# Decays inside a chunk as products of token-major gates with 0/1 matrices, and GpSimd's tile work of the first stage on other engines

## The chip, the cores and the metric

The kernel runs on one core of one Trainium2 chip. A core has TensorE (PE; its weight loads are listed apart as PEld), VectorE (DVE), ScalarE (ACT), GpSimd (POOL) and SyncE (SP), which issues the DMAs. What counts is the device time of one execution in microseconds. A time is compared as the median of several runs; a trace shows one profiled execution.

## The reference

One layer of an encoder trunk on 2048 tokens of width 1024, all in float32. The change lies in the GLA half of the token mixer and in the projection ahead of it:

```python
xn = rms_norm(h, norm_mix_pre[i])
z = xn @ w_in[i]
...
z_rwkv = z_rwkv + rwkv_mu[i] * (centred_shift(z_rwkv) - z_rwkv)
...
log_a = jax.nn.log_sigmoid(jnp.einsum('btdr,drc->btdc', a_lo, a_up) + a_b) / GLA_GATE_TEMP
...
bc = jnp.cumsum(to_chunks(log_a), axis=-2)
def step(S, inp):
    q_c, k_c, v_c, b_c = inp
    o_inter = jnp.einsum('bhcd,bhde->bhce', q_c * jnp.exp(b_c), S)
    diff = b_c[:, :, :, None, :] - b_c[:, :, None, :, :]
    dmat = jnp.exp(jnp.where(mask, diff, -jnp.inf))
    scores = jnp.einsum('bhid,bhjd,bhijd->bhij', q_c, k_c, dmat)
    o_intra = jnp.einsum('bhij,bhje->bhie', scores, v_c)
```

There are 4 GLA heads with 64 key and 128 value channels, and two directions. An RWKV-7 mixer with 8 heads runs beside them; an output projection, a SwiGLU network and a gated embedding follow.

## The kernel before

`phase_a` is the first stage. It goes over the sequence in four quarters of 512 tokens. For each it normalizes and transposes `x` (`make_xn`), then makes 27 column blocks of the projection (`zmat`): each block is 2 x 8 steps of three float32r products (high and low parts, lines 73 to 75), evacuated by ScalarE as `z`. In the first quarter the raw weights `wr` come in halves, ScalarE rounds them to `wh` and GpSimd subtracts to get `wl` (line 218); both go to DRAM, and the later quarters load them from there (line 209).

`mixed` adds a block's neighbours in time (GpSimd, line 296) and mixes them in (VectorE, lines 297 and 298). `rwkv_pair` makes the operands of two RWKV heads, `gla` and `gla_head` those of the GLA heads. A tile of a GLA head holds the forward direction on partitions 0 to 63 and the backward one on 64 to 127. `b` is the running sum of the gates in chunks of 128 tokens. The scores inside a chunk are built in seven levels: at a level with blocks of `n` tokens the decays are `exp` of the distance of `b` from its value in the middle of a block of 2n. GpSimd makes the two differences (532, 533; 523, 524 at level 6), ScalarE the exponential (534), GpSimd multiplies with the queries (`qq`, 535), VectorE with the keys (`kz`, 536, 537), TensorE makes four 128x128 float32 products (`pl`, 540), and VectorE copies them into `sc` under a mask (544).

The generators of the two kinds of heads are interleaved by `ORDER`; within that a scheduler sets the order of each engine's queue when the program is built, and each engine then runs its queue in that order. So products of the projection (`pz`) stand between the small products of the heads. The heads of the last quarter run beside the beginning of `phase_b`, the RWKV recurrence; `phase_c` has the output projection and the rest. GpSimd also computes a triangular inverse at the beginning of `phase_b` (694, 695).

Of the kernel before, what the change touches and what calls it, by code (L numbers as in the profile page):

```python
# [7 lines left out]
F32 = mybir.dt.float32  # L8
# [4 lines left out]
ALU = mybir.AluOpType  # L13
# [75 lines left out]
def col(k, i, n=1):  # L89
    return k.pv[:, i:i + n]  # L90


def phase_a(ctx, ctr, ctb, tc, k):
# [103 lines left out]

    kz = [c.tile([128, TQ], F32, name=f"kz{li}") for li in range(7)]
# [5 lines left out]
    def weights(ft, first):  # L204
# [141 lines left out]
    def rwkv_pair(q, p, x, lo):  # L346
# [30 lines left out]
        sq = t("sq")  # L377
# [27 lines left out]
        for d in range(2):  # L405
# [6 lines left out]
            V.tensor_scalar(u, u, 1.0, None, op0=ALU.add)  # L412
# [29 lines left out]
    def gla(q, x, al):  # L442
        ts_ = slice(q * TQ, q * TQ + TQ)
        t = lambda tag, bufs=1, n=TQ: gp.tile([128, n], F32, tag=tag, bufs=bufs, name=tag)
        for i in range(2):

            ab = abp.tile([128, 2, TQ], F32, tag="ab", name="ab")
            bx = gp.tile([128, 2, TQ], F32, tag="bx", name="bx")
            for hh in range(2):
# [3 lines left out]
                S.activation(ab[:, hh], pg, AF.Abs, bias=col(k, PV_AB + h))  # L453
# [3 lines left out]
            for hh in range(2):  # L457
                V.tensor_sub(ab[:, hh], bx[:, hh], ab[:, hh])

                V.tensor_tensor_scan(bx[0:64, hh], m128[0:64], ab[0:64, hh], 0.0, op0=ALU.mult, op1=ALU.add)  # L460
                V.tensor_tensor_scan(bx[64:128, hh, ::-1], m128[64:128, ::-1], ab[64:128, hh, ::-1], 0.0, op0=ALU.mult, op1=ALU.subtract)
# [11 lines left out]
            for hh in range(2):  # L473
# [6 lines left out]
                gla_head(q, h, bx[:, hh], q2[hh], k2[hh], vt)  # L480
# [8 lines left out]
    def gla_head(q, h, b, q2, k2, vt):  # L489
# [8 lines left out]
        nc.sync.dma_start(k.d["qb"][h, :, q * TQ:q * TQ + TQ], qh[B_])  # L498
        kh = t("f", 2)
# [9 lines left out]

        sc = t("sc")  # L510
        for li in (6, 0, 1, 2, 3, 4, 5):
            pl = ps3.tile([128, 512], F32, tag="ps3", name="pl")
            n = LV[li]
            tv = lambda ap: ap.rearrange("p (b t) -> p b t", t=2 * n)
            nb = TQ // (2 * n)
            bv, k2v, kv = tv(b), tv(k2), tv(kz[li])
            lhs = kz[li]
            rhs = t("qq", 2)
            f = t("f", 2)
            if li == 6:  # L520

                fv = tv(f)
                G.tensor_sub(fv[F_], bv[F_], bv[F_, :, 0:1].to_broadcast([64, nb, 2]))
                G.tensor_sub(fv[B_], bv[B_, :, 1:2].to_broadcast([64, nb, 2]), bv[B_])
                S.activation(f, f, AF.Exp, scale=0.0625)
                G.tensor_mul(rhs, f, q2)
                V.tensor_copy(kv[F_, :, 0:1], k2v[F_, :, 0:1])
                V.tensor_copy(kv[B_, :, 1:2], k2v[B_, :, 1:2])
            else:
                mid = bv[:, :, n:n + 1].to_broadcast([128, nb, n])  # L530
                fv = tv(f)
                G.tensor_sub(fv[:, :, 0:n], mid, bv[:, :, 0:n])
                G.tensor_sub(fv[:, :, n:2 * n], bv[:, :, n:2 * n], mid)
                S.activation(f, f, AF.Exp, scale=0.0625)  # L534
                G.tensor_mul(rhs, f, q2)  # L535
                V.tensor_mul(kv[F_, :, 0:n], fv[F_, :, 0:n], k2v[F_, :, 0:n])
                V.tensor_mul(kv[B_, :, n:2 * n], fv[B_, :, n:2 * n], k2v[B_, :, n:2 * n])  # L537
# [1030 lines left out]
```

## Time and profile before

| | before |
|---|---|
| median of 3 runs | 3658.14 us (3655.13 to 3660.93) |
| profiled execution | 3649.02 us, span 3647.3 us |
| TensorE busy | 3347.8 us (92%) |
| VectorE busy | 2624.4 us (72%) |
| ScalarE busy | 1640.8 us (45%) |
| GpSimd busy | 978.7 us (27%) |
| first stage, about 40 to 1190 us | a third of the span |

Busy times come from one execution. A matmul's row has a start and a modelled end; matmuls are pipelined, so that the distance between starts tells what one costs in a row. An instruction that takes longer than another of the same form and engine was held up in itself; a wait stands in front of an instruction and is put down to the one that came last.

### The profile page before, as it was taken

How to read it: one execution, taken by the hardware profiler on the slowest of the kernel's cores; microseconds unless marked ns; L12 is line 12 of the kernel's file. 1: busy time of each engine (PE TensorE's matmuls, PEld its weight loads, DVE VectorE, ACT ScalarE, POOL GpSimd, SP SyncE). 2: the span in 40 equal slices, each digit the busy share in tenths (PEclk: the TensorE clock that was granted, in tenths of full speed). 3: DMA queues.
4: the chain of work that ended last, by engine and by line, in shares of the span. 5: the costliest groups of instructions: out<-in, count | busy, mean ns of one | idle time of the engine just before them, and what ended most of it. 6: DMA issues, size and time to landing. Idle time of an engine off the chain costs nothing.

```text
span 3647.3 us, 57330 instructions
## 1 busy us (share of the span) xinstructions
PE 3347.8 (92%) x20880; PEld 2856.6 (78%) x20880; DVE 2624.4 (72%) x4123; ACT 1640.8 (45%) x3451; POOL 978.7 (27%) x1348
## 2 busy tenths in 40 slices
PE   6888988988889899999969989999999999999998
PEld 6777877877878688898858868888788878787776
DVE  6888788788778467776763467777765566769887
ACT  5454445444444555656644453333433333324554
POOL 6854534534335144547401100000000000001112
PEclk9988999999998989999979999999999999999999
DMA  6655465465555445545255655555422234557775
GB/s 219 215 189 184 147 199 187 143 197 170 186 177 175 153 133 156 160 130 155 73 159 169 230 200 185 187 193 191 156 93 81 70 115 150 212 173 272 265 272 185
DMA packets 390439, 629.28 MB, mean 173 GB/s; under 512 B 122790, under 2 KB 223142, under 8 KB 390156
## 3 DMA queue, kind: packets, MB, share of 16 engines
q1 hardware_dynamic: 390156, 625.61, 52.3%
q8 instruction: 165, 2.70, 0.3%
q14 instruction: 118, 0.97, 0.1%
HBM read 403.18 MB, written 211.81 MB: 169 GB/s over the span
## 4 chain that ended last, share of the span: by engine, by line
PE 66%; DVE 17%; DMA 6%; ACT 5%; issue 4%; POOL 2%; SPq 1%; DVEq 0%; ACTq 0%; POOLq 0%
PE pB L73 6%; PE pB L75 6%; PE pB L74 6%; PE pA L74 5%; PE pA L75 4%; PE pA L73 4%; PE pC L74 4%; PE pC L75 4%; PE pC L73 4%; PE pg L662 3%; PE ph L781 3%; PE pf L798 2%; PE pz L75 2%; PE pz L73 2%; PE pz L74 2%
## 5 line engine op out<-in xcount | busy, mean ns | idle before, releaser
L1045 ACT CAST sh<-raws 128x512 fp32r<-128x512 f32 (+1 forms) x456 | 277.6, 610 | 667.0 <-PE pB L74 356.2
L73 PE MATMUL pz<-xh,wh 128*128 128x256 f32 (+1 forms) x1728 | 511.8, 297 | 26.7 <-ACT z L291 18.4
L75 PE MATMUL pz<-xh,wl 128*128 128x256 f32 (+1 forms) x1728 | 504.6, 295 | 6.0 <-DMA wl<-d_ws 4.1
L74 PE MATMUL pz<-xl,wh 128*128 128x256 f32 (+1 forms) x1728 | 504.5, 293 | 0.0
L1210 POOL TENSOR_TENSOR st<-st 128x1 f32<-128x1 f32 x64 | 18.0, 281 | 1631.2 <-ACT jk L1209 1630.7
L1046 DVE TENSOR_TENSOR sl<-raws,sh 128x512 fp32r<-128x512 f32 (+1 forms) x456 | 305.6, 671 | 112.9 <-ACT sh L1045 109.4
L73 PEld LDWEIGHTS pz<-xh,wh 128*128 128x128 f32 x1728 | 339.6, 197 | 40.3 <-ACT z L291 29.1
L75 PEld LDWEIGHTS pz<-xh,wl 128*128 128x128 f32 x1728 | 337.9, 197 | 15.1 <-DMA wl<-d_ws 6.8
L74 PEld LDWEIGHTS pz<-xl,wh 128*128 128x128 f32 x1728 | 340.1, 197 | 6.9 <-issue 5.8
L781 PE MATMUL ph<-x,wpi 128*128 128x128 f32 x1024 | 170.7, 295 | 8.9 <-ACT wpi L777 7.4
L73 PE MATMUL pA<-B11h,sh 128*128 128x512 f32 x360 | 147.7, 411 | 23.0 <-ACT B11h L1045 19.1
L540 PE MATMUL pl<-qq,kz 128*128 128x128 f32 x896 | 133.8, 296 | 32.4 <-DVE kz L537 30.9
L798 PE MATMUL pf<-sv,Ht 128*128 128x64 f32 x1024 | 152.3, 277 | 10.7 <-ACT sv L803 6.9
L540 PEld LDWEIGHTS pl<-qq,kz 128*128 128x128 f32 x896 | 121.2, 208 | 44.0 <-issue 30.2
L781 PEld LDWEIGHTS ph<-x,wpi 128*128 128x128 f32 x1024 | 139.8, 200 | 18.2 <-ACT wpi L777 12.9
L798 PEld LDWEIGHTS pf<-sv,Ht 128*128 128x128 f32 x1024 | 136.0, 196 | 22.5 <-ACT sv L803 10.4
L535 POOL TENSOR_TENSOR qq<-f,q 128x512 f32<-128x512 f32 x96 | 140.7, 1472 | 43.5 <-ACT f L534 24.2
L74 PE MATMUL pA<-B11l,sh 128*128 128x512 f32 x360 | 148.1, 411 | 3.3 <-DVE B11l L1046 3.3
L662 PE MATMUL pg<-ar,bk 64*128 64x128 f32 x1024 | 143.4, 297 | 6.0 <-DVE x L665 4.6
L75 PE MATMUL pA<-B11h,sl 128*128 128x512 f32 x360 | 146.7, 407 | 0.9 <-DVE sl L1046 0.9
L73 PE MATMUL pB<-T3h,sh 128*128 128x512 f32 x360 | 143.4, 398 | 0.0
L75 PE MATMUL pB<-T3h,sl 128*128 128x512 f32 x360 | 143.0, 397 | 0.0
(636 smaller groups left out, 9348.5 us busy)
## 6 DMA issues: line engine op xcount, KB each, us to landing
wh<-d_ws SPq DMA_DIRECT2D x81, 512.0 KB, 4.1
wl<-d_ws SPq DMA_DIRECT2D x81, 512.0 KB, 4.8
d_mt<-rawt SPq DMA_DIRECT2D x92, 256.0 KB, 2.5
raws<-in_ffn_gate SPq DMA_DIRECT2D x44, 512.0 KB, 4.4
raws<-in_ffn_up SPq DMA_DIRECT2D x44, 512.0 KB, 4.0
rawm<-d_mt SPq DMA_DIRECT2D x44, 512.0 KB, 8.6
d_hid<-c SPq DMA_DIRECT2D x88, 256.0 KB, 2.5
d_ar<-st SPq DMA_DIRECT2D x32, 512.0 KB, 2.9
```

Of the source, the lines that this page charges most:

```text
L73: nc.tensor.matmul(out, ah, bh, start=start, stop=False, **kw)
L74: nc.tensor.matmul(out, ah, bl, start=False, stop=False, **kw)
L75: nc.tensor.matmul(out, al, bh, start=False, stop=stop, **kw)
L535: G.tensor_mul(rhs, f, q2)
L540: nc.tensor.matmul(pl[:, js], lhs[:, js], rhs[:, js], start=True, stop=True)
L662: nc.tensor.matmul(pg[h][:, j], bk[HR[h], j], ar[HR[h], j], start=True, stop=True)
L781: nc.tensor.matmul(ph[:, h, j], w[:, h, j], x[:, j0 + j, 4 * h:4 * h + 2, :], start=True, stop=True)
L798: nc.tensor.matmul(pf[:, h, j0 + j], H[:, h, j], SV[p, d, c][:, h, j0 + j], start=True, stop=True)
L1045: nc.scalar.copy(hi, src)
L1046: nc.vector.tensor_sub(lo, src, hi.bitcast(F32))
L1210: G.tensor_add(st[:, 2:3], st[:, 0:1], st[:, 1:2])
```

## The change

- The running sum `b` stays for `qh`, `kh` and `dec`. The decays inside the chunk no longer come from it: the gates `g` (tile `ab`) are transposed to token-major form (`gt`, in the buffers of `kt`), and for levels 0 to 5 four products with a 0/1 matrix `W[:, li]` sum the right gates in PSUM (`pf`); ScalarE takes the exponential from there. Level 6 needs one gate alone, beside ones.
- The backward gates stand one column further, with a zero beside them, in a tile of 513 columns. So `Abs` and a subtraction run in halves.
- `decay` is called one level ahead of its use. `kh` and its transposes move behind the levels.
- VectorE makes `qq`, `wl` and the sum of neighbours; ScalarE makes the product with `mu1` and adds 1 to `u`.
- The raw weights have two buffers instead of three; `sq` uses the buffers of `out`.

```diff
+    W = c.tile([128, 6, 128], F32, name="W")
...
+        V.tensor_sub(wv[:, :, 0:n], mid, lv[:, :, 0:n])
+        V.tensor_sub(wv[:, :, n:2 * n], lv[:, :, n:2 * n], mid)
...
-            wr = wp.tile([128, n, 128], F32, tag="wr", bufs=3, name="wr")
+            wr = wp.tile([128, n, 128], F32, tag="wr", bufs=2, name="wr")
...
-            G.tensor_sub(wl[:, js], wr, wh[:, js].bitcast(F32))
+            V.tensor_sub(wl[:, js], wr, wh[:, js].bitcast(F32))
...
-        G.tensor_add(s, z[:, 0:TQ], z[:, 2:TQ + 2])
-        V.tensor_scalar(out, z[:, 1:TQ + 1], mu1[:, i:i + 1], None, op0=ALU.mult)
+        S.activation(out, z[:, 1:TQ + 1], AF.Copy, scale=mu1[:, i:i + 1])
+        V.tensor_add(s, z[:, 0:TQ], z[:, 2:TQ + 2])
...
-        sq = t("sq")
+        sq = t("out", 2)
...
-            V.tensor_scalar(u, u, 1.0, None, op0=ALU.add)
+            S.activation(u, u, AF.Identity, bias=k.one)
...
+            gr = ((slice(0, 64), slice(0, TQ)), (slice(64, 128), slice(1, TQ + 1)))
...
-                S.activation(ab[:, hh], pg, AF.Abs, bias=col(k, PV_AB + h))
+                for r, o in gr:
+                    S.activation(ab[r, hh, o], pg[r], AF.Abs, bias=col(k, PV_AB + h)[r])
...
+        gt = t("kt", 1)
+        tokmajor(g, gt, ps3, "ps3")
+
+        def decay(li):
...
+            pf = ps3.tile([128, 512], F32, tag="ps3", name="pf")
+            for j in range(4):
+                js = slice(128 * j, 128 * j + 128)
+                nc.tensor.matmul(pf[:, js], gt[:, js], W[:, li], start=True, stop=True)
+            f = t("f", 2)
+            S.activation(f, pf, AF.Exp, scale=0.0625)
+            return f
...
+            f = nxt
+            if i < 6:
+                nxt = decay(levels[i + 1])
+            fv = tv(f, n)
+            V.tensor_mul(rhs, f, q2)
...
-                G.tensor_sub(fv[:, :, 0:n], mid, bv[:, :, 0:n])
-                G.tensor_sub(fv[:, :, n:2 * n], bv[:, :, n:2 * n], mid)
-                S.activation(f, f, AF.Exp, scale=0.0625)
-                G.tensor_mul(rhs, f, q2)
```

How the order moves, first on TensorE at the end of the second quarter: the levels of its last head beside the transposes of the next quarter's `x` (`xt`). `v`, `pa`, `pss` belong to an RWKV pair. Before:

```order
L263 MATMUL pt<-ident,xt 128x128 x8
L540 MATMUL pl<-qq,kz_262 128x128 x4
L263 MATMUL pt<-ident,xt 128x128 x4
L540 MATMUL pl<-qq,kz_263 128x128 x4
L263 MATMUL pt<-ident,xt 128x128 x8
L305 MATMUL pt<-ident,v 128x128 x4
L372 MATMUL pa<-ta,aup 128x512
L373 MATMUL pa<-ta,aupl 128x512
L540 MATMUL pl<-qq,kz_264 128x128 x4
```

Now the same place, from the transposes of the gates (`ab`) on:

```order
L315 MATMUL pt<-ident,ab 128x128 x4
L273 MATMUL pt<-ident,xt 128x128 x4
L390 MATMUL pss<-out,bo 128x512
L534 MATMUL pf<-W,kt 128x128 x4
L560 MATMUL pl<-qq,kz_283 128x128 x4
L534 MATMUL pf<-W,kt 128x128 x4
L273 MATMUL pt<-ident,xt 128x128 x4
L560 MATMUL pl<-qq,kz_277 128x128 x4
L534 MATMUL pf<-W,kt 128x128 x4
L560 MATMUL pl<-qq,kz_278 128x128 x4
L534 MATMUL pf<-W,kt 128x128 x4
```

Each level now has a group `pf` ahead, a level earlier than it is used, and the head starts later against the transposes of `x`.

GpSimd's queue in the second quarter, in the middle of a head, before:

```order
L535 TENSOR_TENSOR qq<-f,q_3745 128x512
L296 TENSOR_TENSOR s<-z 128x512
L532 TENSOR_TENSOR f<-bx 128x32x8
L533 TENSOR_TENSOR f<-bx 128x32x8
L535 TENSOR_TENSOR qq<-f,q_3745 128x512 x2
```

And the rest of the second quarter now:

```order
L428 MEMSET E 128x8 x2
L526 MEMSET f 128x512 x2
L428 MEMSET E 128x8 x2
L526 MEMSET f 128x512
L428 MEMSET E 128x8 x3
L246 TENSOR_TENSOR st<-st,mhalf 128x1 x3
```

The sum of neighbours (296) stood between the levels' work; only memsets and the norms' `pow` are left. VectorE's queue at the levels of that last head now:

```order
L550 TENSOR_TENSOR qq<-f,q_5190 128x512
L555 TENSOR_TENSOR kz_279<-f,k_5261 64x16x16
L556 TENSOR_TENSOR kz_279<-f,k_5261 64x16x16
L564 COPY_PREDICATED sc<-msk,pl 128x512
L402 TENSOR_TENSOR P_6460<-kr,ta 64x512
L403 TENSOR_TENSOR P_6459<-kr,ta 64x512
L550 TENSOR_TENSOR qq<-f,q_5190 128x512
```

`qq` stands there in front of the two `kz` of its level; before, a level had two `kz` and the masked copy on this engine.

## Rows read from the trace of the kernel before

**Rows 1.** The page's part 1, and GpSimd's row of part 2.
```profile
PE 3347.8 (92%) x20880; PEld 2856.6 (78%) x20880; DVE 2624.4 (72%) x4123; ACT 1640.8 (45%) x3451; POOL 978.7 (27%) x1348
...
POOL 6854534534335144547401100000000000001112
```

**Rows 2.** Stretches: us; busy PE, PEld, DVE, ACT, POOL (instructions); clock; DMA share; GB/s.
```profile
47.00:341.00 294.00, 246.37 (x1696) 223.56 (x1695) 245.41 (x286) 149.87 (x286) 190.90 (x160) 0.91 0.58 193
341.00:615.00 274.00, 244.72 (x1754) 223.46 (x1753) 219.94 (x302) 127.22 (x244) 119.27 (x116) 0.94 0.55 176
40.00:1130.00 1090.00, 956.32 (x6806) 867.67 (x6804) 874.56 (x1156) 520.03 (x989) 518.41 (x475) 0.94 0.57 184
```

**Rows 3.** Who TensorE waits for, 70 to 1130 us: us, times, longest.
```profile
PE pl L540 <- DVE kz L537: 30.9, 19, 4.5
PE pt L305 <- DVE v L298: 18.6, 6, 5.8
PE pz L73 <- ACT z L291: 17.4, 8, 3.2
...
PE po L557 <- DVE SF L558: 9.3, 8, 2.4
...
PE pz L75 <- POOL wl L218: 1.8, 3, 0.9
...
PE pt L305 <- DVE f L503: 0.2, 1, 0.2
```

**Rows 4.** VectorE, ns min/median/max; last row, 40 to 1130 us: busy us, mean ns.
```profile
L537 DVE TENSOR_TENSOR kz<-f,k x96: 418/423/1452, 94.2 to 1177.8; 64x256 f32<-64x256 f32 x96
...
L297 DVE TENSOR_SCALAR v<-z,mu x16: 486/1010/1414, 118.0 to 1045.0; 128x512 f32<-128x512 f32 x16
...
L402 DVE TENSOR_TENSOR out<-pb,v x16: 676/688/692, 148.9 to 1082.8; 128x512 f32<-128x512 f32 x16
...
L503 DVE TENSOR_TENSOR f<-f,k x16: 659/682/1762, 91.7 to 1139.3; 128x512 f32<-128x512 f32 x16
...
L537 DVE TENSOR_TENSOR kz<-f,k 64x256 f32<-64x256 f32 x88 | 64.8, 736 | 2.5
```

**Rows 5.** GpSimd's groups up to 1500 us: busy us, mean ns | idle before.
```profile
L535 POOL TENSOR_TENSOR qq<-f,q 128x512 f32<-128x512 f32 x96 | 140.7, 1472 | 43.5 <-ACT f L534 24.2 <-PE pl L540 19.1 <-ACT u L411 0.2
...
L532 POOL TENSOR_TENSOR f<-bx 128x256 f32<-128x256 f32 x96 | 88.7, 924 | 123.2 <-PE pt L305 62.2 <-DVE kz L537 59.1
...
L533 POOL TENSOR_TENSOR f<-bx 128x256 f32<-128x256 f32 x96 | 78.8, 821 | 0.0
```

**Rows 6.** TensorE in order of time: start us, us.
```profile
151.19 0.28 PE L75 MATMUL pz<-xh,wl 128*128 128x258 f32 x1
151.31 1.06 PE L540 MATMUL pl<-qq,kz 128*128 128x128 f32 x8
152.12 0.48 PE L408 MATMUL pu<-tw,wup 128*128 128x512 f32 x1
...
664.37 0.41 PE L73 MATMUL pz<-xh,wh 128*128 128x256 f32 x1
664.58 0.36 PE L74 MATMUL pz<-xl,wh 128*128 128x256 f32 x1
...
665.24 0.60 PE L305 MATMUL pt<-ident,qk 128*128 128x128 f32 x4
665.60 0.36 PE L73 MATMUL pz<-xh,wh 128*128 128x256 f32 x1
665.80 0.28 PE L74 MATMUL pz<-xl,wh 128*128 128x256 f32 x1
```

**Rows 7.** A scaled pass of ScalarE, ns min/median/max.
```profile
L435 ACT ACTIVATE cv<-z,pv x32: 706/722/728, 63.5 to 1123.7; 128x512 f32<-128x512 f32 x32
```

**Rows 8.** The raw weights' loads, us to landing; SyncE's wait for them: us, times, longest.
```profile
wr<-in_w_in SPq DMA_DIRECT2D x45, 256.0 KB, 3.8
...
SPq L216 <- POOL wl L218: 25.0, 18, 5.2
```

More of the change, by code (lines that the diff above doesn't have):

```diff
@@ L196, in phase_a @@
         prev = cur
+    W = c.tile([128, 6, 128], F32, name="W")
+    L = pp.tile([128, TQ], F32, tag="u", bufs=2, name="L")[:, :128]
+    G.memset(L, 1.0)
+    G.affine_select(L, L, pattern=[[1, 128]], compare_op=ALU.is_ge, fill=0.0, base=0, channel_multiplier=-1)
+    for li in range(6):
+        n = LV[li]
+        lv, wv = L.rearrange("p (b t) -> p b t", t=2 * n), W[:, li].rearrange("p (b t) -> p b t", t=2 * n)
+        mid = lv[:, :, n:n + 1].to_broadcast([128, 64 // n, n])
+        V.tensor_sub(wv[:, :, 0:n], mid, lv[:, :, 0:n])
+        V.tensor_sub(wv[:, :, n:2 * n], lv[:, :, n:2 * n], mid)
     kz = [c.tile([128, TQ], F32, name=f"kz{li}") for li in range(7)]
@@ L498, in gla_head @@
         nc.sync.dma_start(k.d["qb"][h, :, q * TQ:q * TQ + TQ], qh[B_])
+        sc = t("sc")
+        tv = lambda ap, n: ap.rearrange("p (b t) -> p b t", t=2 * n)
+        gt = t("kt", 1)
+        tokmajor(g, gt, ps3, "ps3")
+        def decay(li):
+            if li == 6:
+                f = t("f", 2)
+                G.memset(f, 1.0)
+                fv = tv(f, 1)
+                S.activation(fv[F_, :, 1:2], g[F_, 0:TQ].rearrange("p (b t) -> p b t", t=2)[:, :, 1:2], AF.Exp, scale=0.0625)
+                S.activation(fv[B_, :, 0:1], g[B_, 1:TQ + 1].rearrange("p (b t) -> p b t", t=2)[:, :, 0:1], AF.Exp, scale=0.0625)
+                return f
[3 more added lines that the diff above has]
+                nc.tensor.matmul(pf[:, js], gt[:, js], W[:, li], start=True, stop=True)
+            f = t("f", 2)
+            S.activation(f, pf, AF.Exp, scale=0.0625)
+            return f
+        levels = (6, 0, 1, 2, 3, 4, 5)
+        nxt = decay(levels[0])
+        for i, li in enumerate(levels):
+            n = LV[li]
+            k2v, kv = tv(k2, n), tv(kz[li], n)
+            lhs = kz[li]
+            rhs = t("qq", 2)
+            f = nxt
[3 more added lines that the diff above has]
+            V.tensor_mul(rhs, f, q2)
+            if li == 6:
+                V.tensor_copy(kv[F_, :, 0:1], k2v[F_, :, 0:1])
+                V.tensor_copy(kv[B_, :, 1:2], k2v[B_, :, 1:2])
+            else:
+                V.tensor_mul(kv[F_, :, 0:n], fv[F_, :, 0:n], k2v[F_, :, 0:n])
+                V.tensor_mul(kv[B_, :, n:2 * n], fv[B_, :, n:2 * n], k2v[B_, :, n:2 * n])
+            pl = ps3.tile([128, 512], F32, tag="ps3", name="pl")
+            for j in range(4):
+                js = slice(128 * j, 128 * j + 128)
+                nc.tensor.matmul(pl[:, js], lhs[:, js], rhs[:, js], start=True, stop=True)
+            if li == 6:
+                V.tensor_tensor(w4(sc), w4(pl), mk7, op=ALU.mult)
+            else:
+                V.copy_predicated(w4(sc), msk[:, li, :].unsqueeze(1).to_broadcast([128, 4, 128]), w4(pl))
         kh = t("f", 2)
@@ L508, in gla_head @@
         tokmajor(kh, kt, ps3, "ps3")
[L510 to L524, printed above, removed]
-                S.activation(f, f, AF.Exp, scale=0.0625)
-                G.tensor_mul(rhs, f, q2)
[L527 to L531, printed above, removed]
-                G.tensor_sub(fv[:, :, 0:n], mid, bv[:, :, 0:n])
-                G.tensor_sub(fv[:, :, n:2 * n], bv[:, :, n:2 * n], mid)
[L534 to L537, printed above, removed]
-            for j in range(4):
-                js = slice(128 * j, 128 * j + 128)
-                nc.tensor.matmul(pl[:, js], lhs[:, js], rhs[:, js], start=True, stop=True)
-            if li == 6:
-                V.tensor_tensor(w4(sc), w4(pl), mk7, op=ALU.mult)
-            else:
-                V.copy_predicated(w4(sc), msk[:, li, :].unsqueeze(1).to_broadcast([128, 4, 128]), w4(pl))
         po = ps3.tile([128, 512], F32, tag="ps3", name="po")
```

15 lines of the change are left out of this document (9 added, 6 removed).

## The prediction

> **What bounds the kernel now.** I read the page first: TensorE is busy for 92% of the span, VectorE for 72%, GpSimd for 27% [rows 1]. The slices show where GpSimd works: before slice 20 [rows 1], and the first thirteen are the stage that the diff touches. So the question is local: what is one microsecond of GpSimd, VectorE or TensorE worth in the first stage?
>
> The second view is the table of stretches. The stage runs four quarters of 512 tokens; where the tile `tw` is made, a new one begins: the first takes 294 us, the second 274. In the second TensorE is busy 244.7 us and VectorE 219.9, which is 89% and 80%; GpSimd 119 us, ScalarE 127 us [rows 2]. Over 40 to 1130 us it is TensorE 956 and VectorE 875 of 1090 us [rows 2]. Nobody has much room, and the time is longer than either engine's work: 134 us in which TensorE does nothing.
>
> The third view is who TensorE waits for. The list from 70 to 1130 us has 19 entries and makes 131 us: the 12 that end with a VectorE instruction (`kz`, `v`, `sc`, `qk`, `SF`, `s` and so on) make 96 us, the 7 that end with ScalarE, a DMA or GpSimd make 35 us, GpSimd itself 1.8 [rows 3]. So GpSimd hardly ever is the one waited for. It hurts through VectorE.
>
> How, the fourth view shows: shortest, median and longest of the same instruction. `kz` on half the partitions takes 418 ns at its shortest and 1452 at its longest; `v` by `mu` 486, with a median of 1010; `f` times `k` 659 to 1762. An instruction with one operand in PSUM, `pb` times `v`, stays between 676 and 692 [rows 4]. The stretching is that of instructions that read SBUF only, while GpSimd streams SBUF too. Summed over all VectorE groups from 40 to 1130 us (busy time less count times the shortest), it is 219 us; the group `kz` of line 537 alone has 64.8 us for 88 where 88 x 0.418 = 37 would do [rows 4]. A quarter of VectorE's time is thus stretching.
>
> **The change part by part.** *TensorE gains work.* Each GLA head (16 of them) gets six groups of four products `pf` and one group of four transposes of the gates. Four `pl` products of the same shape and type stand from 151.31 to 152.12, when the next begins: 0.81 us. Four transposes stand from 665.24 to 665.60: 0.36 us [rows 6]. 96 x 0.81 + 16 x 0.36 = 78 + 6 = 84 us. Behind a group the next `pz` product needs 0.20 us to its successor instead of 0.12 [rows 6]: at most 112 x 0.08 = 9 us more. I take +88 us, on a queue in order that is 89% full.
>
> *GpSimd loses* lines 535, 532, 533, 218, 296 and the level 6 forms, some 500 us [rows 5]. What stays is a memset of 512 columns for each head, the small memsets of `E`, the `pow` of the norms and the inverses of the next stage.
>
> *VectorE gains and loses.* Without stretching, 112 `qq` at the median of `f` times `k`, 0.68 us, are 76 us; 54 `wl` at that price 37 us, the 60 sums of neighbours 41 us. The 60 products with `mu1` leave, 60 x 0.48 = 29 us (shortest of `v` by `mu`), so do 32 additions of one, 13 us if one costs the 0.42 of the shortest `kz` (an estimate); the gates' subtraction in halves adds 16 x 0.68 = 11 us. Together +123 us. Against this up to 219 us of stretching end. 875 - 219 + 123 = 779 us: VectorE falls from 80% to about 71% of the same time.
>
> *ScalarE gains* 60 products and 32 additions at the price of a scaled 128x512 pass, 0.72 us [rows 7], 16 more `Abs` passes and 16 evacuations of the gates: 124 x 0.72 = 89 us as an upper bound. From 520 us to 609 of 1090 [rows 2]: 56%, so it covers it. Where it doesn't is `z`: TensorE waits for ScalarE's copies of `z` 17 us now [rows 3].
>
> *What goes and what is late next.* The places are those in the order above. In GpSimd's queue the sums of neighbours stood behind three microseconds of level work; now only memsets stand there. On VectorE the level has `qq`, two `kz` and the masked copy, about 0.68 + 2 x 0.42 + 0.69 = 2.2 us (the copy reads PSUM, so I price it like `pb` times `v`) [rows 4], where GpSimd needed 0.92 + 0.82 + 1.47 = 3.2 us for its three alone [rows 5]. A level's chain loses 1 us, but gets a product, and with `decay` one level ahead the chain product, `Exp`, `qq` is hidden by the products of the level before. If that cover fails, each level stands for a product, a pass and a `qq`, 0.81 + 0.72 + 0.68 = 2.2 us.
>
> The new matmul `pf` waits for `kt`, the evacuated gates, and behind it the `pz` products of the projection stand in TensorE's queue. The level 6 product, which needs no `pf`, and products of the projection lie between them in the order. I cost this wait at nothing; its bound is one evacuation for each head, 16 x 0.72 = 12 us [rows 7].
>
> *First quarter.* The raw weights get two buffers instead of three, and `wl` moves to VectorE. A half lands 3.8 us after its issue; with a cast and a subtraction of 0.7 us each that is 5.2 us for a pair, where the quarter uses up one pair in 294 / 27 = 10.9 us. So it is covered unless the subtraction stands for over 5 us in VectorE's queue. SyncE waits 25 us for `wl` here already, with three buffers [rows 8]; I take 0 and keep +25 us for the range. `sq` now shares the two buffers of `out` and so waits until `g` is stored; between the two lie the transposes of `v` and the product `pa`, and ScalarE, which would stand there, is free for more than half of its time [rows 2]: nothing.
>
> *The sum.* +88 us of TensorE. Of the 96 us behind VectorE I let three fifths go, 58 us: VectorE's load falls only from 80 to 71%, but what makes its queue late, stretched instructions and the level chain through GpSimd, goes altogether; the waits for `SF` (9 us) are a chain through TensorE itself and stay. The ends are 0 and 96. TensorE's clock is at 0.94 of full over the stage [rows 2]; at the lower level of 1.2 GHz two `pz` products are 0.21 us apart and at 2.4 GHz 0.12 [rows 6]. A denser TensorE should get some of that back; I take 10 us of the 65 that 6% of 1090 us make; the ends are 0 and 30. 88 - 58 - 10 = **+20 us**. The later stages have no edit. The profiled execution took 3649.0 us, the median of the runs is 3658.1, 9 us above it; on the median I predict **3678 us**.
>
> **The rivals.** *A, faster: VectorE was the bound.* Then all 96 us go, and 88 - 96 - 10 = -18 us: 3640 us, or 3620 with all of the clock's 30. For it: 96 of the 131 us of TensorE's waits end with VectorE [rows 3], and a quarter of VectorE's time is waste [rows 4]. Against it: TensorE would have to be busy for (956 + 88) / (1090 - 18), 97% of a stage in which none of the stretches read has 90% [rows 2], and the 35 us of other waits stay.
> The Trainium skill has a rule that points to A (Perfetto Trace Analysis, Identifying the Most-Contended Engine): matmul busy time is a poor measure of the headroom on TensorE, and the busy share of weight loads is to be read instead. By it the second quarter would be 82% full, not 89 [rows 2], and 88 us would fit into what is free. The trace speaks against using it here: `pz` products stand 0.12 us apart, one behind the other [rows 6], so where TensorE has work its queue has no gaps to fill, whatever the weight loads show.
>
> *B, clearly slower: the waits don't fall.* They could be latencies of chains in a fixed order rather than a queue on VectorE: TensorE's queue is in order, and each added group is one more place where it can stand behind a chain. It decides if VectorE's instructions come out short and yet TensorE's idle time stays above 120 us. The price is the whole of +88 us: 3746 us. For it: `v`, `sc` and `SF` are such chains. Against it: `kz` and `v`, which come out stretched, head the list [rows 3, 4].
>
> *C, the change doesn't do what it says: the stretching isn't GpSimd's.* Then VectorE has to carry +123 us without relief and is the bound: up to 3780 us. Against it stands `pb` times `v`, which isn't stretched [rows 4].
>
> **How the numbers follow.** Forecast (TensorE takes over, half to two thirds of VectorE's waits go): 0.50, with a range of its own of 3655 to 3705. A: 0.28. B: 0.16. C and the first quarter's buffers: 0.06. What a measurement of this kernel can tell from no change is 0.2%, 7 us. Faster is A and a little of the forecast's lower end: 0.31. Within 0.2%: 0.15. Slower: 0.54. For 8 in 10 the range reaches to the middle of A and two thirds of the way to B: 3632 to 3722 us.
>
> **What would show it.** GpSimd under 100 us from 40 to 1130 us. VectorE's `kz` at a mean below 0.45 us, and VectorE at about 780 us in the stage. TensorE about 1040 us busy in a stage of about 1110, at 93 to 94%, and its waits behind VectorE near 40 us. Products `pf` in groups of 0.8 us. Wrong it would be if TensorE's waits fell below 50 us in all (A), or if they stayed above 120 with short VectorE instructions (B), or if the first quarter alone grew.

## The result, and the profile after

The changed kernel takes 3594.6 us (median of four runs, 3588.7 to 3629.9) against 3659.5 for the kernel before beside it: a ratio of 0.984, with a 95% interval of 0.981 to 0.988. That is 65 us faster, where 20 us slower was forecast, and 37 us below the low end of the range. The profiled execution took 3591.0 us (span 3589.3), against 3649.0.

The page of the changed kernel, parts 1 and 2, answers to [rows 1]:

```profile
PE 3390.1 (94%) x21712; PEld 2913.7 (81%) x21712; DVE 2543.3 (71%) x4301; ACT 1726.9 (48%) x3595; POOL 456.1 (13%) x916
...
POOL 2000000000002154645211100000000000001112
```

GpSimd is all but gone from the first stage. Next the stretches of the stage, with the columns of [rows 2]. A quarter begins at the first `tw` of ScalarE; the stage ends at the last `ot` (the output of a GLA head, evacuated by ScalarE), at 1196.3 us before and 1151.7 after. Before:

```profile
47.20:345.20 298.00, 250.37 (x1726) 227.17 (x1725) 249.61 (x292) 151.36 (x290) 191.94 (x161) 0.91 0.58 193
345.20:614.90 269.70, 240.42 (x1722) 219.55 (x1721) 215.64 (x296) 125.43 (x242) 118.22 (x115) 0.94 0.55 175
40.00:1196.30 1156.30, 1017.36 (x7154) 919.28 (x7152) 926.99 (x1259) 546.24 (x1041) 554.34 (x533) 0.94 0.56 181
```

After:

```profile
44.00:303.70 259.70, 244.87 (x1873) 226.68 (x1872) 210.90 (x349) 168.30 (x317) 6.64 (x17) 0.99 0.67 226
303.70:575.10 271.40, 261.70 (x2016) 243.36 (x2016) 206.38 (x346) 153.06 (x289) 7.88 (x21) 0.99 0.55 177
40.00:1151.70 1111.70, 1065.29 (x8053) 978.33 (x8052) 856.31 (x1460) 639.60 (x1199) 37.30 (x104) 0.99 0.58 191
```

Three things are to be read here. TensorE is busy for 1065 of 1112 us, 96%. The granted clock is 0.99 of full instead of 0.94. And the first quarter, where GpSimd had worked for 192 of 298 us, is 38 us shorter, while the second is 2 us longer: there the products cost about what the relief gave.

Who TensorE waits for, 70 to 1152 us, answers to [rows 3] (us in all, times, longest):

```profile
PE pl L560 <- DVE kz L556: 12.5, 9, 3.9
PE pz L75 <- DVE wl L228: 9.1, 5, 4.5
PE pz L75 <- DMA wl<-d_ws: 7.5, 8, 1.8
...
PE pf L534 <- ACT kt L316: 1.2, 3, 0.5
PE pz L73 <- ACT z L301: 1.1, 2, 0.6
...
PE po L587 <- DVE SF L588: 0.3, 1, 0.3
```

The whole list is 46 us in the changed kernel, 29 of them behind VectorE. For the kernel before, read to its own last `ot`, it is 137 us, 100 of them behind VectorE. The wait of the new products for the evacuated gates (`pf` behind `kt`) is 1.2 us.

VectorE's durations after, ns shortest/median/longest, answer to [rows 4]:

```profile
L555 DVE TENSOR_TENSOR kz<-f,k x96: 398/411/550, 101.0 to 1134.3; 64x256 f32<-64x256 f32 x96
L556 DVE TENSOR_TENSOR kz<-f,k x96: 422/422/439, 101.4 to 1134.7; 64x256 f32<-64x256 f32 x96
...
L412 DVE TENSOR_TENSOR out<-pb,v x16: 684/692/694, 137.0 to 1018.0; 128x512 f32<-128x512 f32 x16
```

The stretching has all but ended: the longest `kz` went from 1.45 us to 0.55, and the product with an operand in PSUM, which was never stretched, is as it was.

One view of the kernel before stands in neither the rows nor the prediction, ScalarE's waits, 70 to 1196 us:

```profile
ACT f L534 <- POOL f L533: 132.8, 58, 6.1
ACT f L525 <- POOL f L524: 14.4, 5, 6.7
```

So GpSimd was waited for, by ScalarE's `Exp` of the decays, for 147 us. In the changed kernel all that is left of this is 5.1 us behind a memset.

At the start of the first inverse of the next stage the changed kernel is 74 us ahead (1107.3 us against 1181.4); at the start of the last of the eight it is 59.5 ahead (1714.0 against 1773.5), and 58 at the end. The stages without an edit thus give 16 us back.

### The profile page after: what moved, and what is told of

It is laid out like the page before. It is cut to its first block, busy times and chain, and to the rows that moved or that the text cites. A ratio compares the mean times of both kernels' runs of the same rounds, so it can differ in the third digit from the quotient of the medians.

```text
span 3589.3 us, 58707 instructions
## 1 busy us (share of the span) xinstructions
PE 3390.1 (94%) x21712; PEld 2913.7 (81%) x21712; DVE 2543.3 (71%) x4301; ACT 1726.9 (48%) x3595; POOL 456.1 (13%) x916
## 4 chain that ended last, share of the span: by engine, by line
PE 57%; DVE 5%; DMA 5%; ACT 2%; issue 2%; SPq 1%; POOL 0%; DVEq 0%; ACTq 0%; POOLq 0%
PE pB L73 6%; PE pB L75 6%; PE pB L74 6%; PE pA L74 5%; PE pA L75 5%; PE pA L73 4%; PE pC L74 4%; PE pC L75 4%; PE pC L73 4%; PE pg L692 3%; PE ph L811 3%; PE pf L828 2%; PE pt L803 1%; PE pt L698 1%; PE pt L1257 1%
## 5 line engine op out<-in xcount | busy, mean ns | idle before, releaser
L75 PE MATMUL pz<-xh,wl 128*128 128x256 f32 (+1 forms) x1728 | 495.4, 290 | 16.6 <-DVE wl L228 9.1
L75 PEld LDWEIGHTS pz<-xh,wl 128*128 128x128 f32 x1728 | 328.7, 192 | 24.5 <-DVE wl L228 10.2
L73 PEld LDWEIGHTS pz<-xh,wh 128*128 128x128 f32 x1728 | 330.7, 191 | 16.5 <-issue 9.8
L74 PEld LDWEIGHTS pz<-xl,wh 128*128 128x128 f32 x1728 | 331.4, 192 | 7.9 <-issue 7.2
L74 PE MATMUL pB<-T3l,sh 128*128 128x512 f32 x360 | 142.5, 396 | 0.0
L807 ACT COPY wpi<-pt 64x256 f32<-64x256 f32 x256 | 93.8, 366 | 89.2 <-PE pt L803 85.0
L1075 ACT CAST sh<-s 128x512 fp32r<-128x512 f32 (+1 forms) x76 | 46.3, 609 | 187.3 <-PE pA L74 163.8
```

The costliest lines, as they stand in the source:

```text
L73: nc.tensor.matmul(out, ah, bh, start=start, stop=False, **kw)
L74: nc.tensor.matmul(out, ah, bl, start=False, stop=False, **kw)
L75: nc.tensor.matmul(out, al, bh, start=False, stop=stop, **kw)
L807: S.copy(w[HR[h], h], pt[HR[h], 2:4])
L1075: nc.scalar.copy(hi, src)
```

## The experiments

Three theories were tried. **Q**: GpSimd's streaming stretches VectorE's instructions; TensorE waits for those, and its clock falls with the waits. **L**: the gain comes from the products, which take the decays out of the level's chain and one level ahead. **K**, formed after the first four runs: GpSimd was a slow link in chains that TensorE waits for, whatever it does to VectorE's durations. All ratios are to the kernel before on the same chip. The stage is always 40 us to the last `ot`; its rows have the columns of [rows 2].

### Only the moves, without the products

```
-                G.tensor_sub(fv[:, :, 0:n], mid, bv[:, :, 0:n])
+                V.tensor_sub(fv[:, :, 0:n], mid, bv[:, :, 0:n])
...
-                G.tensor_mul(rhs, f, q2)
+                V.tensor_mul(rhs, f, q2)
...
-        G.tensor_add(s, z[:, 0:TQ], z[:, 2:TQ + 2])
-        V.tensor_scalar(out, z[:, 1:TQ + 1], mu1[:, i:i + 1], None, op0=ALU.mult)
+        S.activation(out, z[:, 1:TQ + 1], AF.Copy, scale=mu1[:, i:i + 1])
+        V.tensor_add(s, z[:, 0:TQ], z[:, 2:TQ + 2])
...
-            G.tensor_sub(wl[:, js], wr, wh[:, js].bitcast(F32))
+            V.tensor_sub(wl[:, js], wr, wh[:, js].bitcast(F32))
```

> The kernel before with GpSimd's tile work of the first stage on VectorE and ScalarE, but the decays still as differences (VectorE makes them too, 96 x 2 halves and 16 x 2 at level 6); no product pf. Theory Q (the gain is VectorE's: GpSimd stretched its instructions, the waits behind it went and TensorE's clock rose with them): kz near 0.43 us, VectorE about 875 - 219 + 112 + 105 = 870 us in the stage, TensorE without the 88 us of the products; 3545 to 3600 us. Theory L (the gain is the level chain: products one level ahead instead of differences, exponential and multiplication in a row): 3635 to 3665 us, as before.

Measured: 3577.9 us, ratio 0.977 (0.973 to 0.980). This beats both kernels: the products are not what gains. The stage:

```profile
40.00:1093.50 1053.50, 984.83 (x7215) 896.13 (x7214) 910.64 (x1615) 618.16 (x1149) 35.83 (x89) 0.97 0.61 201
```

It is 103 us shorter than before and 58 shorter than after. (Of the whole kernel's time the products cost less than that: by the two ratios 0.8%, 28 us; the last section shows where the rest goes.) VectorE carries the differences and yet is busy for 911 us, less than the 927 of before, since next to nothing is stretched.

### Only the products, the other work back on GpSimd

```
-            V.tensor_mul(rhs, f, q2)
+            G.tensor_mul(rhs, f, q2)
...
-            V.tensor_sub(wl[:, js], wr, wh[:, js].bitcast(F32))
+            G.tensor_sub(wl[:, js], wr, wh[:, js].bitcast(F32))
```

(the sums, the products with `mu1` and the additions of one go back too; against the changed kernel).

> The changed kernel with qq, wl and the sum of neighbours back on GpSimd, mu1's product and the addition of one back on VectorE; the decays stay products, a level ahead. Theory Q: GpSimd works for some 300 us in the stage, half of the stretching stays, and TensorE has its 88 us more: 3640 to 3700 us. Theory L: the chain is short all the same: 3595 to 3620 us.

Measured: 3678.9 us, ratio 1.004 (1.001 to 1.007). So the products, with the differences off GpSimd and the rest of its work still there, gain nothing; L falls. GpSimd is busy for 347 us of the stage, and the wait for `kz` is back:

```profile
PE pl L560 <- DVE kz L556: 40.2, 29, 3.2
```

### Idle GpSimd work beside the changed kernel

Products of `f` with `q2` and `k2`, of `wh` with itself and of `z` with its neighbour, into a tile that nobody reads:

```
+            stir(f, q2)
+            stir(f, k2)
...
+    def stir(u, v):
+        for o in (0, 256):
+            G.tensor_tensor(noise, u[:, o:o + 256], v[:, o:o + 256], op=ALU.mult)
```

> The changed kernel with idle work for GpSimd: it multiplies tiles that lie there anyway (the rounded weights, z, the decays f with q and k) into a scratch tile that nobody reads, some 430 us in the stage. Nothing waits for a result; f, z and the weights are held a little longer. Theory Q: the stretching comes back (kz at a mean of 0.6 to 0.75 us, VectorE up by 100 to 200 us), TensorE's waits behind VectorE and the lower clock too: 3650 to 3720 us. Theory L: 3590 to 3610 us.

Measured: 3850.4 us, ratio 1.051 (1.048 to 1.055). `kz` has a mean of 0.84 and 0.75 us on the two halves, TensorE's waits are 199 us and the clock 0.93. That is far over Q's range. But part of it is another thing: `f` has two buffers, and the next `f` waited for the idle reader (ScalarE 25 us). So it was repeated with `q2` and `k2` in place of `f`:

```
-            stir(f, q2)
-            stir(f, k2)
+            stir(q2, k2)
+            stir(q2, q2)
```

> The changed kernel, with GpSimd work that nobody waits for: beside each level two products of q2 and k2 or q2 with itself into a scratch tile, beside each sum of neighbours and each half of raw weights the like. Nothing is read from f, whose two buffers were held in the run before of this kind. Theory Q (GpSimd's streaming beside VectorE stretches VectorE's instructions, and TensorE then waits for them): kz at a mean over 0.55 us, TensorE's waits over 90 us, and at least +40 us against the changed kernel, a ratio to the kernel before of 0.996 or more. Theory K (GpSimd cost time because it was a slow link in chains that TensorE waits for, whatever it does to VectorE's durations): kz may come out long, but the time stays within 10 us of the changed kernel, a ratio of 0.982 to 0.988.

Measured: 3745.9 us, ratio 1.024 (1.019 to 1.029): 4.0% or 145 us more than the changed kernel, and 86 us above the kernel before. The stage:

```profile
40.00:1290.20 1250.20, 1116.15 (x8165) 1007.79 (x8165) 1025.34 (x1465) 640.57 (x1201) 627.51 (x776) 0.96 0.52 171
```

Its two `kz` groups (busy us, mean ns):

```profile
L565 DVE TENSOR_TENSOR kz<-f,k 64x256 f32<-64x256 f32 x96 | 59.9, 624 | 0.0
L566 DVE TENSOR_TENSOR kz<-f,k 64x256 f32<-64x256 f32 x96 | 55.1, 574 | 1.4
```

And who TensorE waits for first:

```profile
PE pl L570 <- DVE kz L566: 54.6, 34, 5.8
```

All that Q said of it came. But GpSimd was again late for others: ScalarE waited 25 us for a memset of level 6 and 15 us for `wh`, so stretching is not the only thing in these 145 us.

### TensorE's side: every group of `pf` twice

```
+            for j in range(4):
+                js = slice(128 * j, 128 * j + 128)
+                nc.tensor.matmul(pf[:, js], gt[:, js], W[:, li], start=True, stop=True)
```

> The changed kernel with each group of four products pf made twice into the same bank (the second overwrites the first): 96 x 0.81 = 78 us more for TensorE, nothing for another engine but the delay. If TensorE is the bound after the change: 3655 to 3675 us. If it still has room (waits that the products can fill): 3600 to 3635 us.

Measured: 3679.1 us, ratio 1.004 (1.001 to 1.007). Against the changed kernel that is 1.9%, 70 us for 96 groups, 0.73 us for one; the prediction's price was 0.81. The time itself is 4 us over the upper range. The stage:

```profile
40.00:1229.60 1189.60, 1148.43 (x8867) 1063.83 (x8867) 861.39 (x1462) 641.38 (x1195) 38.66 (x104) 0.98 0.54 178
```

It is 78 us longer with 83 us more of TensorE, at 97% busy: after the change TensorE is the bound, and a group costs it nearly what the +88 us term had for it.

### The moves one at a time

From here on the edits are to the kernel before. First `wl` alone, then the sums (with the products by `mu1` and the additions of one on ScalarE) alone, as in the diff of the first experiment:

> The kernel before with one of the moves: wl, the difference of the raw weights and their rounded form, on VectorE. GpSimd loses 54 x 1.5 = 81 us, nearly all in the first quarter, VectorE gains 54 x 0.7 = 37. Theory Q: the first quarter loses 81 of its 190 us of GpSimd work, so its stretching falls by some two fifths (34 of 86 us); against 37 us of added work that is about nothing on VectorE: ratio 0.993 to 1.001. Theory K: TensorE waits for wl itself 1.8 us; what stood behind wl in GpSimd's queue comes earlier: ratio 0.993 to 0.998, the gain in the first quarter.

> The kernel before with one of the moves: the 60 sums of neighbours on VectorE, and the 60 products with mu1 and the 32 additions of one from VectorE to ScalarE. GpSimd loses some 60 to 70 us, VectorE gains 41 and loses 42. Theory Q: no more load on VectorE, some 28 us less stretching: ratio 0.990 to 0.995. Theory K: the waits for v and xt fall (TensorE waits 19 us for them in the kernel before): 10 to 20 us, ratio 0.994 to 0.997; below 0.990 the sums were a link whose price the list of waits doesn't show.

Measured: `wl` 3644.3 us, ratio 0.996 (0.994 to 0.998); the sums 3649.4 us, 0.998 (0.995 to 1.001). `wl` lies in the ranges of both theories, and the sums gain less than either had, if anything. So these two decide little. Then the level's differences and `qq` alone:

> The kernel before with one of the moves: the level's differences and qq on VectorE. GpSimd loses some 330 us, VectorE gains 96 x (2 x 0.42 + 0.68) = 146 us. Theory Q: two thirds of the stretching goes, some 140 of 219 us, against 146 of added work: about nothing on VectorE, ratio 0.994 to 1.004. Theory K: the level's chain before its products falls from 3.2 us on GpSimd and 0.8 on VectorE to 2.4 in one queue; TensorE's 31 us of waits for kz go for the most part: ratio 0.988 to 0.994. If the three moves together make less than the 0.977 of all of them at once, they depend on each other.

Measured: 3558.4 us, ratio 0.971 (0.966 to 0.977), more than either theory allowed: this one move is worth more than the whole change, and at least as much as all moves together.

```profile
40.00:1123.40 1083.40, 1000.54 (x7223) 906.29 (x7221) 951.13 (x1600) 553.67 (x1056) 185.84 (x199) 0.96 0.60 196
```

TensorE's wait for `kz`, 30.9 us before [rows 3]:

```profile
PE pl L540 <- DVE kz L537: 19.4, 15, 4.0
```

Two groups of VectorE (busy us, mean ns; before, `qq` was GpSimd's and `kz` had 736 ns [rows 4]):

```profile
L535 DVE TENSOR_TENSOR qq<-f,q 128x512 f32<-128x512 f32 x96 | 69.3, 722 | 3.5 <-ACT f L534 3.3
L537 DVE TENSOR_TENSOR kz<-f,k 64x256 f32<-64x256 f32 x96 | 50.8, 529 | 1.6
```

VectorE is now busy for 951 of 1083 us, 88%, where it had 80% before, and still TensorE waits less (81 us in all instead of 137). Load on VectorE was the wrong measure. (The profiled execution, 3584.9 us, is the slowest of this kernel's four, the others lie between 3548 and 3564; so the stage's rows show less than the median gained.) With `wl` added:

> The kernel before with two of the moves: the level's differences and qq, and wl, on VectorE; the sums of neighbours stay on GpSimd, and there are no products for the decays. If the moves add up (0.971 for the levels alone, 0.996 for wl alone): a ratio of 0.964 to 0.971. If wl's 37 us on VectorE cost what they save now that the levels are there too: 0.971 to 0.977, as with all three moves.

Measured: 3559.6 us, ratio 0.973 (0.970 to 0.977). So the moves don't add up: apart they make 2.9 + 0.4 + 0.2 = 3.5%, together 2.3%. Once the level work is off GpSimd, `wl` and the sums bring nothing more that these runs can tell. These two versions and the first experiment lie within each other's intervals; all three are faster than the changed kernel.

### Stretching or a slow link: idle work on the kernel with the levels moved

The kernel of the levels alone, with the same kind and amount of work put back on GpSimd for nobody:

```
+            G.tensor_tensor(noise[:, 0:8], kz[li][:, 0:8], kz[li][:, 0:8], op=ALU.mult)
+            nv = noise.rearrange("p (b t) -> p b t", t=n)
+            for o in (0, n):
+                G.tensor_sub(nv, k2v[:, :, o:o + n], k2v[:, :, n:n + 1].to_broadcast([128, nb, n]))
+            for o in (0, 256):
+                G.tensor_mul(noise, k2[:, o:o + 256], q2[:, o:o + 256])
```

> The kernel before with the level work on VectorE, and in its place on GpSimd the same kind and amount of work (two differences and two half products for each level, on k2 and q2, started by the level's kz) into a scratch tile that nobody reads. Theory Q (stretching): VectorE's kz comes out long again, TensorE's waits go from 80 us back over 115, and most of the 2.9% is lost: a ratio of 0.990 to 1.005. Theory K (slow link): nobody waits for this work, so the gain stays: a ratio of 0.968 to 0.978.

Measured: 3699.8 us, ratio 1.011 (1.008 to 1.015): the gain is lost and more, 4.0% or 146 us, and the time lies over Q's range. Its stage:

```profile
40.00:1247.80 1207.80, 1036.63 (x7215) 931.82 (x7214) 1087.27 (x1601) 552.22 (x1057) 634.82 (x759) 0.93 0.54 176
```

TensorE's first two waits:

```profile
PE pl L547 <- DVE kz L538: 47.3, 24, 4.8
PE pl L547 <- DVE qq L536: 29.6, 19, 4.1
```

The same two groups of VectorE:

```profile
L536 DVE TENSOR_TENSOR qq<-f,q 128x512 f32<-128x512 f32 x96 | 75.2, 783 | 3.4 <-ACT f L535 3.2
L538 DVE TENSOR_TENSOR kz<-f,k 64x256 f32<-64x256 f32 x96 | 57.5, 599 | 2.3
```

For 1600 instructions each, VectorE's busy time is 951 us without and 1087 with the idle work: 136 us of stretching. ScalarE has no wait behind GpSimd here, TensorE 0.8 us, and SyncE, which loads the next `q2` and `k2`, 4 us behind the idle work. So hardly anybody waits for it, and it costs more than moving the level work had gained. A new order of the queues, which a scheduler makes for each program, isn't the reason: from 30 us to 60 us before the stage's end, 98% of VectorE's instructions and 98% of TensorE's stand at the same place of their queue as with the levels alone.

Is it the reading, or that GpSimd is busy at all? First the idle work of the changed kernel as fills:

```
+        G.tensor_tensor(noise[:, 0:8], u[:, 0:8], v[:, 0:8], op=ALU.mult)
+        for _ in range(6):
+            G.memset(noise, 0.0)
```

> The changed kernel with idle GpSimd work at the places of the run that read q2, k2, z and wh, but as fills: each pair of products is six memsets of 128x256 behind a product of 8 columns, so that GpSimd is busy for some 400 to 600 us more and reads nothing. If GpSimd's reading is what stretches VectorE: ratio 0.982 to 0.990, kz's mean below 0.45 us. If its writing does it as well: in proportion to its busy time, 1.005 to 1.03.

Measured: 3705.5 us, ratio 1.013 (1.010 to 1.017), with no stretching of `kz`: it has its 0.41 and 0.43 us.

```profile
L567 DVE TENSOR_TENSOR kz<-f,k 64x256 f32<-64x256 f32 x96 | 40.8, 425 | 1.4
```

The ratio lies in the range that was expected if writing stretches too, but `kz` came out as short as it was expected if only reading does: the time was lost in another way, which neither expectation had. GpSimd is busy for 778 us and late, and ScalarE waited for what it held or had to do:

```profile
ACT f L537 <- POOL f L535: 22.6, 7, 6.0
ACT wh L233 <- POOL noise L214: 15.5, 3, 7.5
ACT wh L233 <- POOL noise L216: 12.5, 4, 5.5
```

TensorE in turn waited for ScalarE:

```profile
PE pz L73 <- ACT wh L233: 32.4, 6, 9.0
```

So the run didn't decide, and the fills were put where nothing is held: on the kernel of the levels alone, started by `kz` as in the run with idle products:

```
+            G.tensor_tensor(noise[:, 0:8], kz[li][:, 0:8], kz[li][:, 0:8], op=ALU.mult)
+            for _ in range(14):
+                G.memset(noise, 0.0)
```

> The kernel before with the level work on VectorE, and GpSimd kept as busy as in the run with idle differences and products (some 600 us in the stage), started at the same places by the level's kz, but with fills of the scratch tile that read nothing; no tile that another engine needs is held. Theory Q (it is VectorE's stretching, which fills did not cause): kz's mean stays near 0.5 us as with the levels alone, TensorE's waits stay under 100 us, ratio 0.966 to 0.980. Theory K (it is the full GpSimd queue, in front of the sums, wl and the norms): as with the idle differences and products, 1.00 or more.

Measured: 3584.1 us, ratio 0.980 (0.975 to 0.984). The stage:

```profile
40.00:1129.40 1089.40, 1000.50 (x7216) 905.24 (x7215) 955.99 (x1599) 553.54 (x1056) 697.86 (x1846) 0.96 0.60 195
```

The same two groups of VectorE:

```profile
L536 DVE TENSOR_TENSOR qq<-f,q 128x512 f32<-128x512 f32 x96 | 71.3, 743 | 3.1 <-ACT f L535 2.7
L538 DVE TENSOR_TENSOR kz<-f,k 64x256 f32<-64x256 f32 x96 | 50.0, 520 | 2.1
```

GpSimd is busier than with the products (698 us against 635), VectorE's time stays at 956 us, and of the 146 us some 30 are left (the interval overlaps that of the levels alone). The other 115 or so go with the reads and VectorE's 131 us; the order of VectorE's queue differs more here (71% at the same place as with the levels alone).

The Trainium skill has this rule (SBUF — State Buffer, SBUF: two separate sides): VectorE and GpSimd share a pair of ports, one instruction holds it whole, and a VectorE instruction with two inputs in SBUF is concerned only by a GpSimd instruction that reads SBUF. These runs agree: 1087 us of VectorE beside GpSimd's reads, 956 beside its fills.

### A microsecond of VectorE

The kernel of the levels alone, with two half products more in VectorE's own queue for each level:

```
+            for o in (0, 256):
+                V.tensor_mul(noise, k2[:, o:o + 256], q2[:, o:o + 256])
```

> The kernel before with the level work on VectorE, and two half products of k2 and q2 more on VectorE for each level, into a scratch tile: some 80 us of short instructions in its queue. It prices VectorE's time by itself. Theory Q (VectorE is a queue that TensorE waits for): a quarter to a half of it comes out as time, 20 to 45 us, a ratio of 0.977 to 0.984. If VectorE's load alone were the bound: all of it, 0.993. If its load cost nothing and only GpSimd's part in the chains had mattered: at most 0.974.

Measured: 3599.8 us, ratio 0.984 (0.981 to 0.988): 1.3%, 47 us, a little over Q's half. The added group, and the stage:

```profile
L540 DVE TENSOR_TENSOR noise<-k,q 128x256 bf16<-128x256 f32 x224 | 102.1, 456 | 1.7
```

```profile
40.00:1152.30 1112.30, 1009.07 (x7224) 912.21 (x7223) 1021.31 (x1819) 560.26 (x1060) 199.68 (x199) 0.95 0.58 191
```

VectorE's busy time rose by 70 us net, so one microsecond costs 0.7. Of stretching it cost 146 / 136 = 1.1. By the intervals of the ratios these are 0.3 to 1.0 and 0.9 to 1.25. That a long instruction in the middle of a level's chain is worse than a short one more at its end would fit, but is not shown: the added products also changed the order of VectorE's queue (15% of its other instructions at the same place).

### The link alone

VectorE's added load of the moved level work is 96 x (2 x 0.44 + 0.72) = 154 us (the two differences at 0.44, `qq` at 0.72), and yet its busy time rose by 24 us only; so 130 us of stretching went. At 0.7 us for added load and 1.1 for stretching that would be a gain of 35 us, not 105, though within the intervals of the two prices it could be anything from a loss to the whole 105. The slow link was the candidate for the rest. Here it is put back on the kernel of the levels alone, ahead of the `Exp` and ahead of the products, with 8 columns of the tile and fills in between:

```
+    def link(x):
+        G.tensor_tensor(noise[:, 0:8], x[:, 0:8], x[:, 0:8], op=ALU.mult)
+        for _ in range(3):
+            G.memset(noise, 0.0)
+        G.tensor_tensor(x[:, 0:8], x[:, 0:8], k.one.to_broadcast([128, 8]), op=ALU.mult)
...
+                link(f)
                 S.activation(f, f, AF.Exp, scale=0.0625)
                 V.tensor_mul(rhs, f, q2)
+                link(rhs)
```

> The kernel before with the level work on VectorE, and GpSimd put back into the level's chain without the tile's data: between VectorE's differences and the Exp, and between qq and its products, GpSimd reads 8 columns, fills a scratch tile three times and multiplies 8 columns by one in place, some 1.7 us each time, as long as the differences and qq took it before. No stretching comes of fills; what is added is the slow link. If the link was worth nothing (Q alone): as with free fills, a ratio of 0.974 to 0.984. If the link was worth what a balance of the runs leaves over (105 us gained by moving the levels, some 35 of it by stretching less VectorE's added load): ratio 0.986 to 0.996, with ScalarE waiting over 100 us for GpSimd.

Measured: 3567.4 us, ratio 0.976 (0.972 to 0.979). The link is there, as ScalarE's and TensorE's waits show:

```profile
ACT f L544 <- POOL f L207: 148.4, 62, 5.7
```

```profile
PE pl L551 <- POOL qq L207: 29.2, 22, 5.9
```

But it costs 0.4%, 16 us, and the intervals overlap: from nothing to some 40 us. TensorE's waits are 85 us in all, 5 more than without it: the products now wait for GpSimd's `qq` where they had waited for `kz`. So K falls as the main cause: waits as long as ScalarE's 147 us were worth some 16 us of time, if anything; other products may have lain beside them. (The order of the queues was made anew for this program too, 8% of VectorE's instructions are at the same place; so it prices a link that the order allows for, as the order of the kernel before did.) What is left of the account at the head of this section lies in its prices: perhaps `qq` and differences, moved into a place of the chain where time had been spent anyway, cost less than half products added behind them. That wasn't measured.

## Why the prediction was wrong, step by step

- **The mechanism was right, its sizes were not.** That GpSimd hurts through VectorE's stretched instructions is what the run with idle products shows. The prediction's rival C falls, and of the signs that it named, GpSimd at 37 us and `kz` at 0.41 and 0.42 us came true; TensorE's waits behind VectorE fell to 29 us, not near 40.
- **TensorE's +88 us was about right as work.** Doubling the 96 groups cost 70 us, where 78 was priced for them; the transposes of the gates weren't measured apart. Taking the products out (the moves alone) gave back 58 us of the stage and 28 of the whole time.
- **The step that failed is the size of the waits.** "Of the 96 us behind VectorE I let three fifths go, 58 us", because "VectorE's load falls only from 80 to 71%". Over the whole stage 91 us of waits went: 71 behind VectorE (100 to 29) and 17 behind ScalarE (24 to 7). The load did not decide: with the levels alone on VectorE it rose to 88% and the waits still fell by 57 us. VectorE itself was read well enough: 927 - 219 + 123 = 831 us on the stage's own ends, against 856 measured, and some 23 us of stretching are left. (Summed again over each line, tile and shape of the trace, the 219 us are 206; from 40 us to the last `ot` it is 212 before, 94 with the levels alone and 23 after.)
- **The waits that "stay" went too.** `z` behind ScalarE fell from 17.4 us [rows 3] to 1.1, `SF` from 9.3 (10.6 up to the last `ot`) to 0.3. They had been counted as latencies of their own, and fell with the rest. ScalarE's 147 us behind GpSimd's differences, which the prediction doesn't have, would not have told it either: put back alone, a wait of that length cost 16 us, if anything.
- **The clock was the larger miss against its term.** "I take 10 us of the 65". The clock went from 0.94 to 0.99: 0.06 x 1156 - 0.01 x 1112 = 58 us (the clock's two digits make this uncertain by some 8). The two belong together: over the runs the stage's clock is lower, loosely, where TensorE waits longer. Without products the waits are 69 us at 0.97; 71, 81, 85 and 87 at 0.96; 101 and 140 at 0.95; 137 at 0.94; 136 and 169 at 0.93. With products they are 46 at 0.99, 41 and 101 at 0.98, 131 at 0.96, 112 at 0.94 and 199 at 0.93. What drives what is not shown by this.
- **The sum with these sizes**: 88 - 91 - 58 = -61 us. As waits and clock go together, adding them as two terms is an estimate. The stage measures -45 up to the last `ot`, by which time the changed kernel has done some 30 us more of the next stage, and -74 up to the first inverse.
- **Rival A** had the direction, and its sign (under 50 us of waits in all: 46) came true, but its 3640 or 3620 us lacked the clock and the other waits. The objection against it, that TensorE would have to be 97% busy where no stretch had 90%, was no objection: it is 96% busy. With only the moves, too, it reaches 93% (985 of 1054 us): the 89% had been no limit of TensorE's.
- The rule of the Trainium skill that was weighed beside A (Perfetto Trace Analysis, Identifying the Most-Contended Engine), that matmul busy time is a poor measure of TensorE's headroom and the busy share of weight loads is to be read, gave A's direction but not by its reason. After the change weight loads are busy for 978 of 1112 us, 88%, and 83 us more of matmul work made the stage 78 us longer. Here the matmuls' busy time, 96%, told better what is free.
- **The first quarter** was costed at 0 with up to +25 us for fewer buffers of raw weights; it became 38 us shorter. TensorE's wait for `wl` did grow, from 1.8 us to 9.1, and did not show against the gain. The new wait for `kt` was rightly costed at nothing, with a bound of 12 us: 1.2 us.

What stays open is a full account of the 105 us that the levels alone gained: idle reads in place of the moved work cost 146 us, for the most part with VectorE's stretching, and the slow link no more than some 40, which makes the stretching the likely largest part; but the price of the load that VectorE took over instead was not measured apart.

## What to carry to other kernels

Before an engine's share of busy time is used to say how much of a wait will go, look whether the same instruction has a shortest and a longest time far apart: here VectorE at 88% with shorter instructions served TensorE better than at 80% with more stretched ones. GpSimd's work that reads SBUF was paid for a second time here, in VectorE's instructions beside it: try it on VectorE first, and only then ask whether TensorE, which was the bound afterwards, should carry any of it. The products were that second step, and the kernel is faster without them. And look at TensorE's waits together with its granted clock, which here rose as they fell. Before a small difference between two programs is explained, compare the order of their queues, since a scheduler makes it anew.

## What the runs showed of the hardware

GpSimd's reading stretches VectorE's two-input instructions that lie in SBUF, and its fills don't, at equal or more busy time (above). An instruction with one input may behave otherwise: VectorE's addition of one, 471 ns on average with the levels alone, took 563 beside fills and 610 beside products (in the stretch from 40 to 1100 us):

```profile
L413 DVE TENSOR_SCALAR u<-u 128x512 f32<-128x512 f32 x32 | 18.0, 563 | 2.3 <-ACT u L412 2.2
```

That row is from the run with fills without held tiles. These are means of some 30 instructions, the longest of them 1.3 to 1.5 us, and GpSimd's `wl` and sums run beside all three, so the difference is not clean. In the changed kernel GpSimd reads next to nothing; there, in the stretch from 40 to 1100 us, one copy with one input is longer beside the fills (second row) than without (first row):

```profile
L553 DVE COPY kz<-k 64x256 f32<-64x256 f32 x16 | 4.7, 291 | 1.1 <-DMA k<-qk 0.8
```

```profile
L564 DVE COPY kz<-k 64x256 f32<-64x256 f32 x14 | 4.8, 345 | 0.9 <-DMA k<-qk 0.5
```

The other one-input groups there hardly change (`ta` 538 and 553 ns, `sg` 428 and 427). The same section of the Trainium skill names VectorE instructions in a two-port mode as the other case, which every GpSimd instruction concerns, reading or not. No row shows the mode; 563 against 471 and 345 against 291 would fit it, `ta` and `sg` would fit it only if they don't run in that mode.

A gain in one stage can be given back in part in another that has no edit. From the first product of the next stage to the final ones, the same 5842 products, before, after, and with only the moves:

```profile
1272.10:1888.60 616.50, 572.09 (x5842) 520.74 (x5842) 448.85 (x1014) 366.38 (x1086) 294.59 (x546) 0.96 0.48 135
```

```profile
1205.90:1831.70 625.80, 584.16 (x5842) 531.86 (x5842) 448.71 (x1014) 366.50 (x1086) 292.49 (x546) 0.94 0.47 133
```

```profile
1152.70:1806.80 654.10, 606.68 (x5842) 551.33 (x5842) 449.71 (x1014) 367.12 (x1086) 292.97 (x546) 0.90 0.45 128
```

The instructions are the same and the granted clock is lower, 0.96, 0.94 and 0.90: the kernel with only the moves lost 38 of its 103 us there, the changed kernel 9. So the products' 58 us of the first stage shrink to some 28 of the whole. With the levels alone, in the slowest execution of its four, the stretch took 645 us at 0.90. What in these kernels lowers the clock in a stage that was not changed is not settled; each profile is one execution.
